# Operand addresses by padding, one merged first load, and a prioritised evacuation in a one-core decoder layer

## Chip, core and metric

The kernel runs on one NeuronCore of a Trainium2 chip. The metric is the device time of one execution in microseconds; several runs of the same kernel are compared by their median.

## What is computed

One decoder layer over 256 tokens of width 2048, all in fp32. A combined projection feeds two attentions (multi-head latent attention with 16 heads, sliding-window attention with 32 query heads and 4 key/value heads), whose outputs are gated, merged and projected; a gated feed-forward with a causal convolution of width 3 follows.

```
h  = RMSNorm_pre(x)
P  = h @ W_in        # 2048 x 7488: q-latent | kv-latent | rope key | q, k, v of the window | two gates
A  = latent attention(P) ; Bq = window attention(P)
y  = W_out( sigmoid(gA) * (A @ Wo_A) + sigmoid(gB) * (Bq @ Wo_B) )
x  = x + RMSNorm_post(y)
x  = x + RMSNorm_post2( ConvFFN( RMSNorm_pre2(x) ) )   # 2048 -> 2 x 5632 -> 2048
```

## The kernel before

Every matrix product is done with three fp32r matmuls. Each operand is split into a high part (a cast to fp32r) and a low part (the remainder), and `mm3` (L144 to L147) issues high x high, low x high and high x low into one PSUM accumulator. The weight is the moving operand (512 columns in most products), the activations are the stationary operand (128 columns: one of two token tiles).

`gemm` (L149) walks the contraction dimension in chunks of two k-tiles of 128 rows (512 KB). For each chunk `wchunk` (L103) issues one DMA on SP's queue into a `raw` buffer (`RAW` = 3 of them), lets ScalarE cast it to `whi` (L120) and VectorE form `wlo` (L121); `whi` and `wlo` have five buffers each (`RING`). Each k-tile then has two token tiles with three matmuls each, so a chunk of two k-tiles is 12 matmuls.

The stationary activations stand in tiles of 128 x 512 fp32r: `ah`/`al` (slots "a": normalised x, later the merged branch and the first 8 of 12 feed-forward tiles), `bh`/`bl` (slots "b": the window attention's output, the latent attention's output, the second normalised x) and `gh`/`gl` (the other four feed-forward tiles, from a later pool). In the down projection (`down`, L902) a product's contraction therefore runs first over `ah`/`al` and then over `gh`/`gl`, with the same weights' buffers as moving operand.

Where a tile stands in SBUF follows from the order in which the pools hand out space. Three dummy tiles shift everything behind them: `line_a` (L233, `LINE_A` columns) stands ahead of slots a, `line_b` (L335) ahead of slots b, `line_w` (L339) ahead of the weights' ring and all later pools. The start addresses in one partition, in bytes, as the built programs have them:

| tiles | first address before, modulo 256 | first address after, modulo 256 |
|---|---|---|
| `ah`, `al` | 21760, 0 | 21984, 224 |
| `bh`, `bl` | 54784, 0 | 55008, 224 |
| `raw`, `whi`, `wlo` | 87936, 128 | 88288, 224 |
| `gh`, `gl` | 191360, 128 | 191712, 224 |
| `cqh`, `ckh`, `qn`, `kn`, `kx` and others of the attentions | 0 | 96 |

Columns within a tile are reached in steps of 512, 1024, 1280 or 2048 bytes, so a slice has the residue of its tile.

The first product (`acc_kv`, L283: keys and values of the window attention) starts while x is still being loaded, in an order written by hand (up to `head.close()`). `load_xt` brings transposed pieces of x (1, 1, 2, 2, ... k-tiles), the first two and the norm scales `gmat` from ScalarE's queue, the others from SP's between the weights. `x_cols` splits each piece into `ah` and `al` with the norm scale, and asks for the next one. Untransposed x comes in four loads `xc`; their sums of squares (`x_square`) give the row factor `r1` (`x_norm`, L274), which is only applied when the accumulators are evacuated (`swa_kv`, L300): ScalarE and VectorE write the keys `kd`, ScalarE the values `vs`. TensorE then turns the values over with `flip` (`swa_v`, tile `vr`, L312) and transposes the keys (`swa_k`, tile `kt`, L319). These steps stand in a list by chunk (`at`, `tick`): `swa_begin` after chunk 2 of the next product, `swa_kv` after 3, `swa_v` after 4 and 5, `swa_k` after 4 to 7. From there on a scheduler orders each engine's instructions by the program's order and by priorities.

Of the kernel before, what the change touches and what calls it, by code (L numbers as in the profile page):

```python
# [19 lines left out]
P = 128  # L20
D = 2048
S = 256
NT = 2
KT = D // P
# [14 lines left out]
GELU_C = math.sqrt(2.0 / math.pi)  # L39


def trunk_layer(ctx, tc, x, x_cols_in, gain_cols, conv_cols_in, g_mix_post, g_ffn_post, w_in, w_q, w_kv,
                sinks, rel, wo_a, wo_b, w_out, w_up, w_down, rope_tab, strip_sel, out):
    nc = tc.nc
    vec, act, pe, pool = nc.vector, nc.scalar, nc.tensor, nc.gpsimd
# [10 lines left out]
    base = ctx.enter_context(tc.tile_pool(name="base", bufs=1))  # L56
    ring = ctx.enter_context(tc.tile_pool(name="ring", bufs=RING))

    def sb(pl, shape, name, dt=F32, tag=None, bufs=None):
        return pl.tile(shape, dt, name=name, tag=tag or name, **({"bufs": bufs} if bufs else {}))  # L60
# [12 lines left out]
    def warm_up(n):  # L73
        for i in range(n):
            tc.keep_in_program_order(pe.matmul(warm[:, 0:P], ident_b, ident_b, start=True, stop=True))

    warm_up(WARM[0])
    causal = sb(base, [P, P], "causal", BF16)
# [10 lines left out]
    gmat = sb(base, [P, 38], "gmat")  # L89
# [13 lines left out]
    def wchunk(src, shape, own=None, rawp=None):  # L103
        i = cnt[0]
        cnt[0] += 1
        n = int(np.prod(shape))
        raw = rawp.tile([P, 1024], F32, name=f"raw{i}", tag="xraw") if rawp else \
            ring.tile([P, 1024], F32, name=f"raw{i}", tag="raw", bufs=RAW)
        dst = raw[:, :n]
        if len(shape) == 2:  # L110
            dst = dst.rearrange("p (a b) -> p a b", a=shape[0])
        elif len(shape) == 3:
            dst = dst.rearrange("p (a b c) -> p a b c", a=shape[0], b=shape[1])
        if len(shape) == 3:
            for k in range(shape[0]):
                nc.sync.dma_start(dst[:, k], src[:, k])
        else:
            nc.sync.dma_start(dst, src)
        hi, lo = ((own or ring).tile([P, 1024], F32R, name=f"w{part}{i}", tag="w" + part) for part in ("hi", "lo"))
        act.copy(hi[:, :n], raw[:, :n])  # L120
        vec.tensor_tensor(lo[:, :n], raw[:, :n], hi[:, :n].bitcast(F32), op=ALU.subtract)  # L121
        return hi, lo
# [5 lines left out]
    def at(t, *fs):  # L128
        steps[max(t, now[0])].extend(fs)

    def tick():
        for f in steps.pop(now[0], ()):
            f()
        now[0] += 1
# [5 lines left out]
    def new_acc(tag):  # L140
        i = cnt[0]
        return [pacc.tile([P, 512], F32, name=f"acc{tag}_{i}_{t}", tag="acc") for t in range(NT)]

    def mm3(o, ah, al, bh, bl, start, stop):  # L144
        pe.matmul(o, ah, bh, start=start, stop=False)  # L145
        pe.matmul(o, ah, bl, start=False, stop=False)  # L146
        pe.matmul(o, al, bh, start=False, stop=stop)  # L147

    def gemm(xh, xl, w, k0, nk, c0, n, split=False, pre=None, extra=None):  # L149

        kc = 1024 // n if n in (256, 512) else 2
        acc = new_acc("g")
        todo = []
        cuts = [0, 1, 2] + list(range(4, nk + 1, 2)) if pre else list(range(0, nk, kc)) + [nk]
        for ci, (k, ke) in enumerate(zip(cuts[:-1], cuts[1:])):
            kk = ke - k
            src = w[(k0 + k) * P:(k0 + k + kk) * P, c0:c0 + n].rearrange("(a p) n -> p a n", p=P)
            if pre and ci == 0:
                pre(k, ke)
            hi, lo = wchunk(src, [kk, n], *(extra or {}).get(ci, ()))  # L160
            if pre and ke < nk:
                pre(ke, cuts[ci + 2])
            for j in range(kk):
                kt = k + j
                wh, wl = hi[:, j * n:(j + 1) * n], lo[:, j * n:(j + 1) * n]
                for t in range(NT):
                    def go(kt=kt, t=t, wh=wh, wl=wl):
                        mm3(acc[t][:, :n], xh(k0 + kt)[:, t * P:(t + 1) * P],
                            xl(k0 + kt)[:, t * P:(t + 1) * P], wh, wl, kt == 0, kt == nk - 1)
                    if split and t == 1:  # L170
                        todo.append(go)
                    else:
                        go()
            tick()
        return acc, todo
# [23 lines left out]
    def split_to(hi, lo, src, scale=None):  # L199

        if scale is None:
            act.copy(hi, src)  # L202
            vec.tensor_tensor(lo, src, hi.bitcast(F32), op=ALU.subtract)
        else:
            act.activation(hi, src, AF.Copy, scale=scale)
            vec.scalar_tensor_tensor(lo, src, scale, hi.bitcast(F32), op0=ALU.mult, op1=ALU.subtract)
# [1 line left out]

    esl, lpool = open_pool("lpool")
    es0, p0 = open_pool("p0")  # L210
    xcut = [0, 1, 2] + list(range(4, KT + 1, 2))
    xr = sb(p0, [P, KT, 256], "xr")

    def load_xt(i, q):
        if i < len(xcut) - 1:
            k, ke = xcut[i], xcut[i + 1]
            q.dma_start(xr[:, k:ke, :], x_cols_in[:, k * 256:ke * 256].rearrange("p (k n) -> p k n", n=256))

    first = sb(base, [P, 1], "first")
    nc.scalar.dma_start(gmat, gain_cols)  # L220
    load_xt(0, nc.scalar)
    load_xt(1, nc.scalar)
    act.copy(first, ident[:, 0:1])
    xc = []

    def load_x():
        c = len(xc)
        t = sb(p0, [P, NT, 512], f"xc{c}")
        nc.sync.dma_start(t, x[:, c * 512:(c + 1) * 512].rearrange("(t p) n -> p t n", p=P))
        xc.append(t)  # L230

    cvT = sb(base, [P, 176], "cvT")
    sb(base, [P, LINE_A], "line_a")  # L233
    xth = [slot_a(p, "h") for p in range(8)]
    xtl = [slot_a(p, "l") for p in range(8)]
    XH, XL = pair_view(xth), pair_view(xtl)
# [9 lines left out]
            act.activation(junk, xc[c][:, t, :], AF.Square, accum_out=ssx[:, t, c:c + 1])  # L246

    def x_cols(k, ke):
        i = xcut.index(k)
        if i:  # L250
            load_xt(i + 1, nc.sync)
        if i in (5, 6, 7):
            load_x()
        if i == 8:
            x_square(0)
        for k in range(k, ke):
            split_to(XH(k), XL(k), xr[:, k, :], gmat[:, k:k + 1])


    strip = dram.tile([SH, 384], F32, name="strip")  # L260
# [13 lines left out]
    def x_norm():  # L274
        vec.tensor_reduce(v1, ssx, axis=AX.X, op=ALU.add)
        vec.tensor_scalar(v1, v1, 1.0 / D, EPS, op0=ALU.mult, op1=ALU.add)
        r = rsqrt(v1, NT, "r1", base)
        vec.tensor_scalar(r1s, r, 0.125, None, op0=ALU.mult)
        vec.tensor_scalar(rh, r, 0.5, None, op0=ALU.mult)
        return r  # L280

    warm_up(WARM[1])
    acc_kv, _ = gemm(XH, XL, w_in, 0, KT, C_KS, 512, pre=x_cols)  # L283
    load_x()
    head.close()

    es1, p1, r1, kx, vx, kd, vs = None, None, None, [], [], [], []

    def swa_begin():
        nonlocal es1, p1, r1
        x_square(3)
        r1 = x_norm()
        es0.close()
        es1, p1 = open_pool("p1")
        kx.extend(sb(p1, [P, 2, 384], f"kx{g}", F32R) for g in range(4))
        vx.extend(sb(p1, [P, 4, 2, 64], f"vx{t}", F32R) for t in range(NT))

    def swa_kv(t):  # L300
        kk = sb(p1, [P, 4, 2, 64], f"kd{t}", tag="qx", bufs=2)
        a3 = acc_kv[t].rearrange("p (a b) -> p a b", b=64)
        act.activation(kk[:, :, 0, :], a3[:, 0:4, :], AF.Copy, scale=r1[:, t:t + 1])
        vec.tensor_scalar(kk[:, :, 1, :], a3[:, 0:4, :], r1[:, t:t + 1], None, op0=ALU.mult)
        v_ = sb(p1, [P, 256], f"vs{t}", tag="p", bufs=3)
        act.activation(v_, acc_kv[t][:, 256:512], AF.Copy, scale=r1[:, t:t + 1])
        kd.append(kk)
        vs.append(v_)

    def swa_v(t):  # L310
        pv_ = pss.tile([P, 512], F32, name=f"vr{t}", tag="s")
        pe.matmul(pv_[:, 0:256], flip, vs[t], start=True, stop=True)  # L312
        o = pv_[:, 0:256].rearrange("p (a b) -> p a b", b=64)
        split_to(vx[t][:, :, 0, :], vx[t][:, :, 1, :], o)
# [13 lines left out]
    at(2, swa_begin)  # L328
    for t in range(NT):
        at(3, lambda t=t: swa_kv(t))  # L330
        at(4 + t, lambda t=t: swa_v(t))
    for g in range(4):
        at(4 + g, lambda g=g: swa_k(g))

# [3 lines left out]
    OH, OL = pair_view(oth), pair_view(otl)  # L338
    sb(base, [P, LINE_W], "line_w")  # L339

# [478 lines left out]
    for b in range(4):  # L819
        c0, n = W_BLOCKS[b]  # L820
# [114 lines left out]
    for b in range(NB):  # L935
        c0, n = blocks[b]
# [15 lines left out]


RING = 5
WARM = (12, 15)
EXTRA = 3
LINE_A = 24
LINE_B = 32
LINE_W = 8
RAW = 3  # L960
STG = 4

# [27 lines left out]
def _columns(a):  # L990

    return np.asarray(a).reshape(-1, P).T
# [32 lines left out]
```

## Time and profile before

| | us |
|---|---|
| median of 3 runs | 1524.61 (1523.99 to 1525.87) |
| the profiled execution's own time | 1525.49 |
| its span, first to last instruction | 1523.7 |
| TensorE busy in it (matmuls) | 1507.3 |
| VectorE busy, ScalarE busy | 940.2, 799.8 |
| mean granted TensorE clock | 0.998 |

Matmuls overlap their neighbours in the trace: a matmul's own duration says less than the distance from one start to the next. That distance is read from a stretch's length and its number of weight loads, one for each matmul.

### The profile page before, as it was taken

What the parts mean: (1) busy time and instruction counts of PE and PEld (TensorE: products, weight loads), DVE (VectorE), ACT (ScalarE), POOL (GpSimd) and SP (SyncE); (2) the same over time, 40 slices, a digit from 0 to 9 for tenths busy, and PEclk for the clock granted to TensorE, in tenths of its full rate; (3) what the DMA queues carried; (4) which work ended last, traced back from release to release, by engine and by line L of the source; (5) the groups of instructions that cost most, each with busy time, mean ns of one, the idle gap of its engine ahead of it and who ended that gap; (6) DMA issues with size and microseconds to landing.
All of it is one profiled execution on the core that took longest, in us unless ns stands there. A gap on an engine that the chain in (4) does not pass through costs nothing.

```text
span 1523.7 us, 20082 instructions
## 1 busy us (share of the span) xinstructions
PE 1507.3 (99%) x7311; PEld 1246.1 (82%) x7311; DVE 940.2 (62%) x1603; ACT 799.8 (52%) x1290; POOL 59.1 (4%) x99
## 2 busy tenths in 40 slices
PE   9999999999999999999999999999999999999997
PEld 7788888888889888888888888888888888888887
DVE  6688884445676665655766656666444466656755
ACT  6588874434565553444655545555443455545542
POOL 1022200000000010000000000000000000000000
PEclk9999999999999999999999999999999999999999
DMA  9776566666655558766555566655556665655563
GB/s 302 209 188 170 146 187 184 205 205 197 180 162 148 176 175 306 240 203 194 175 186 179 179 185 187 179 180 181 186 189 193 184 184 180 184 180 180 180 192 112
DMA packets 162979, 287.55 MB, mean 189 GB/s; under 512 B 18613, under 2 KB 34261, under 8 KB 162752
## 3 DMA queue, kind: packets, MB, share of 16 engines
q1 hardware_dynamic: 157440, 269.78, 57.5%
q0 software_dynamic: 5008, 16.21, 4.2%
q8 instruction: 57, 0.93, 0.2%
q14 instruction: 42, 0.34, 0.1%
q10 hardware_dynamic: 432, 0.28, 0.1%
HBM read 279.89 MB, written 6.34 MB: 188 GB/s over the span
## 4 chain that ended last, share of the span: by engine, by line
PE 94%; DVE 2%; ACT 2%; DMA 1%; issue 1%; DVEq 0%; ACTq 0%; SPq 0%
PE accg L145 28%; PE accg L146 28%; PE accg L147 28%; PE fT L850 1%; DMA raw<-in_w_in_dram 1%; PE mpo L684 1%; PE ms L650 1%; DVE wlo L121 1%; PE qn L613 0%; PE qn L615 0%; PE qn L614 0%; ACT p L410 0%; PE pt L368 0%; PE ms L655 0%; ACT whi L120 0%
## 5 line engine op out<-in xcount | busy, mean ns | idle before, releaser
L121 DVE TENSOR_TENSOR wlo<-raw,whi 128x1024 fp32r<-128x1024 f32 (+2 forms) x501 | 609.0, 1217 | 509.6 <-ACT whi L120 509.3
L120 ACT CAST whi<-raw 128x1024 fp32r<-128x1024 f32 (+2 forms) x501 | 522.1, 1043 | 616.5 <-PE accg L147 528.8
L145 PE MATMUL accg<-whi,bh 128*128 128x512 f32 x960 | 382.6, 399 | 0.0
L147 PE MATMUL accg<-whi,bl 128*128 128x512 f32 x960 | 379.1, 395 | 0.0
L146 PE MATMUL accg<-wlo,bh 128*128 128x512 f32 x960 | 379.0, 395 | 0.0
L145 PE MATMUL accg<-whi,ah 128*128 128x512 f32 (+2 forms) x896 | 347.8, 389 | 1.1 <-ACT whi L120 1.1
L146 PE MATMUL accg<-wlo,ah 128*128 128x512 f32 (+2 forms) x896 | 345.8, 386 | 0.0
L147 PE MATMUL accg<-whi,al 128*128 128x512 f32 (+2 forms) x896 | 344.9, 385 | 0.0
L147 PEld LDWEIGHTS accg<-whi,bl 128*128 128x128 f32 x960 | 180.4, 188 | 43.0
L146 PEld LDWEIGHTS accg<-wlo,bh 128*128 128x128 f32 x960 | 180.6, 188 | 41.1
L145 PEld LDWEIGHTS accg<-whi,bh 128*128 128x128 f32 x960 | 180.5, 188 | 40.8
L147 PEld LDWEIGHTS accg<-whi,al 128*128 128x128 f32 x896 | 169.3, 189 | 35.1
L145 PEld LDWEIGHTS accg<-whi,ah 128*128 128x128 f32 x896 | 169.4, 189 | 33.7 <-ACT whi L120 1.4
L146 PEld LDWEIGHTS accg<-wlo,ah 128*128 128x128 f32 x896 | 169.4, 189 | 33.6 <-DVE wlo L121 0.7
L145 PE MATMUL accg<-whi,gh 128*128 128x512 f32 (+1 forms) x104 | 39.4, 378 | 0.0
L146 PE MATMUL accg<-wlo,gh 128*128 128x512 f32 (+1 forms) x104 | 38.8, 373 | 0.0
L147 PE MATMUL accg<-whi,gl 128*128 128x512 f32 (+1 forms) x104 | 38.4, 374 | 0.0
L410 ACT ACTIVATE p<-p,nm 128x128 f32<-128x128 f32 x64 | 28.3, 445 | 5.8 <-DVE nm L401 5.8
L850 PEld LDWEIGHTS fT<-ident,f 128*128 128x128 f32 x176 | 21.9, 141 | 6.0
L850 PE MATMUL fT<-ident,f 128*128 128x128 f32 x176 | 26.4, 272 | 0.0
L854 ACT ACTIVATE cc<-fT,cvT 128x256 f32<-128x256 f32 x44 | 24.3, 553 | 0.0
L145 PEld LDWEIGHTS accg<-whi,gh 128*128 128x128 f32 x104 | 19.6, 188 | 4.1 <-ACT gh L202 0.8
(289 smaller groups left out, 1265.6 us busy)
## 6 DMA issues: line engine op xcount, KB each, us to landing
raw<-in_ffn_w_up_dram SPq DMA_DIRECT2D x176, 512.0 KB, 4.1
raw<-in_w_in_dram SPq DMA_DIRECT2D x111, 512.0 KB, 4.3
raw<-in_ffn_w_down_dram SPq DMA_DIRECT2D x88, 512.0 KB, 3.8
raw<-in_w_o_swa_dram SPq DMA_DIRECT2D x32, 512.0 KB, 4.1
raw<-in_w_o_mla_dram SPq DMA_DIRECT2D x32, 512.0 KB, 4.5
raw<-in_w_out_dram SPq DMA_DIRECT2D x32, 512.0 KB, 4.0
raw<-in_mla_w_q_up_dram SPq DMA_DIRECT2D x48, 128.0 KB, 2.6
bias<-strip POOLq DMA_DIRECT2D x16, 256.0 KB, 3.9
```

The lines of the kernel that those rows point to most:

```text
L120: act.copy(hi[:, :n], raw[:, :n])
L121: vec.tensor_tensor(lo[:, :n], raw[:, :n], hi[:, :n].bitcast(F32), op=ALU.subtract)
L145: pe.matmul(o, ah, bh, start=start, stop=False)
L146: pe.matmul(o, ah, bl, start=False, stop=False)
L147: pe.matmul(o, al, bh, start=False, stop=stop)
L410: act.activation(pb[:, i, a:b], pb[:, i, a:b], AF.Exp, bias=st["nm"][:, i, t:t + 1], accum_out=st["sm"][:, i, t:t + 1])
L650: pe.matmul(o, w, v_, start=n == 0, stop=False)
L684: pe.matmul(o, w(t), p_[:, c], start=n == 0, stop=n == 5)
L850: pe.transpose(pt[:, q * 256 + t * P:q * 256 + (t + 1) * P], sa[t][q][:, i * P:(i + 1) * P], ident)
L854: act.activation(cc, a, AF.Identity, scale=w2, bias=cb_)
```

## The change

The pads `LINE_A` and `LINE_W` become larger, which gives the addresses in the table above. The norm scales and the first k-tile of x become one input array and one load (`gx`); `gmat` is copied out of it later by GpSimd. All pieces of x come on SP's queue, in the order in which they are used; the first six k-tiles of x and of the weight come singly (before: two). The loads `xc` come one piece later. `x_norm` and `swa_kv` get a higher priority, and `swa_v` moves two chunks later (`swa_k` stays where it is).

```diff
-    nc.scalar.dma_start(gmat, gain_cols)
-    load_xt(0, nc.scalar)
-    load_xt(1, nc.scalar)
+    gx = sb(p0, [P, 38 + 256], "gx")
+    xr = [sb(p0, [P, ke - k, 256], f"xr{k}") for k, ke in zip(XCUT[1:-1], XCUT[2:])]
+    def load_xt(i):
+        if i == 0:
+            nc.sync.dma_start(gx, x_cols_in[:, 0:38 + 256])
+        elif i < len(XCUT) - 1:
+            k, ke = XCUT[i], XCUT[i + 1]
+            nc.sync.dma_start(xr[i - 1], x_cols_in[:, 38 + k * 256:38 + ke * 256].rearrange("p (k n) -> p k n", n=256))
+    load_xt(0)
...
     def x_cols(k, ke):
-        i = xcut.index(k)
-        if i:
-            load_xt(i + 1, nc.sync)
-        if i in (5, 6, 7):
+        i = XCUT.index(k)
+        for j in {0: (), 1: (1, 2)}.get(i, (i + 1,)):
+            load_xt(j)
+        if i in X_AT:
             load_x()
-        if i == 8:
+        if i == len(XCUT) - 2:
             x_square(0)
-        for k in range(k, ke):
-            split_to(XH(k), XL(k), xr[:, k, :], gmat[:, k:k + 1])
+        for j in range(k, ke):
+            src = xr[i - 1][:, j - k, :] if i else gx[:, 38:]
+            split_to(XH(j), XL(j), src, gx[:, j:j + 1])
...
     load_x()
+    pool.tensor_copy(gmat, gx[:, 0:38])
     head.close()
...
-        r1 = x_norm()
+        with tc.high_priority(300):
+            r1 = x_norm()
...
     def swa_kv(t):
+        with tc.high_priority(300):
+            swa_evac(t)
+
+    def swa_evac(t):
...
-        at(4 + t, lambda t=t: swa_v(t))
+        at(6 + t, lambda t=t: swa_v(t))
...
+XCUT = [0, 1, 2, 3, 4, 5, 6, 8, 10, 12, 14, 16]
+X_AT = (8, 9, 10)
-LINE_A = 24
+LINE_A = 80
 LINE_B = 32
-LINE_W = 8
+LINE_W = 40
```

More of the change, by code (lines that the diff above doesn't have):

```diff
@@ L39, with trunk_layer @@
 GELU_C = math.sqrt(2.0 / math.pi)
-def trunk_layer(ctx, tc, x, x_cols_in, gain_cols, conv_cols_in, g_mix_post, g_ffn_post, w_in, w_q, w_kv,
+def trunk_layer(ctx, tc, x, x_cols_in, conv_cols_in, g_mix_post, g_ffn_post, w_in, w_q, w_kv,
                 sinks, rel, wo_a, wo_b, w_out, w_up, w_down, rope_tab, strip_sel, out):
@@ L153, in gemm @@
         todo = []
-        cuts = [0, 1, 2] + list(range(4, nk + 1, 2)) if pre else list(range(0, nk, kc)) + [nk]
+        cuts = XCUT if pre else list(range(0, nk, kc)) + [nk]
         for ci, (k, ke) in enumerate(zip(cuts[:-1], cuts[1:])):
@@ L210, in trunk_layer @@
     es0, p0 = open_pool("p0")
[L211 to L217, printed above, removed]
+    gx = sb(p0, [P, 38 + 256], "gx")
[6 more added lines that the diff above has]
+            nc.sync.dma_start(xr[i - 1], x_cols_in[:, 38 + k * 256:38 + ke * 256].rearrange("p (k n) -> p k n", n=256))
     first = sb(base, [P, 1], "first")
-    nc.scalar.dma_start(gmat, gain_cols)
-    load_xt(0, nc.scalar)
-    load_xt(1, nc.scalar)
+    load_xt(0)
     act.copy(first, ident[:, 0:1])
@@ L1009 @@
         add(name, inputs[name], name != "rel_bias_table")
-    add("x_cols", np.asarray(inputs["x"])[0].T.reshape(KT, P, S).transpose(1, 0, 2).reshape(P, KT * S), False)
-    add("gain_cols", np.concatenate([_columns(inputs[n][0]) for n in
-                                     ("norm_mix_pre", "norm_ffn_pre", "mla_q_norm", "mla_kv_norm")], 1), False)
+    gains = [_columns(inputs[n][0]) for n in ("norm_mix_pre", "norm_ffn_pre", "mla_q_norm", "mla_kv_norm")]
+    cols = np.asarray(inputs["x"])[0].T.reshape(KT, P, S).transpose(1, 0, 2).reshape(P, KT * S)
+    add("x_cols", np.concatenate(gains + [cols], 1), False)
     add("conv_cols", np.concatenate([_columns(inputs["ffn_conv_w"][0]), _columns(inputs["ffn_conv_b"][0])], 1), False)
@@ L1017 @@
     o = nc.dram_tensor("out_0_dram", (1, S, D), F32, kind="ExternalOutput").ap()
-    order = ["x", "x_cols", "gain_cols", "conv_cols", "norm_mix_post", "norm_ffn_post", "w_in", "mla_w_q_up", "mla_w_kv_up",
+    order = ["x", "x_cols", "conv_cols", "norm_mix_post", "norm_ffn_post", "w_in", "mla_w_q_up", "mla_w_kv_up",
              "swa_sinks", "rel_bias_table", "w_o_mla", "w_o_swa", "w_out", "ffn_w_up", "ffn_w_down", "rope_tab", "strip_sel"]
```

## The prediction

> **What bounds the kernel now.** I read the page first, then the groups of TensorE by shape, the table by stretches, the waits of TensorE, and the timeline of the start.
>
> ```profile
> span 1523.7 us, 20082 instructions
> PE 1507.3 (99%) x7311; PEld 1246.1 (82%) x7311; DVE 940.2 (62%) x1603; ACT 799.8 (52%) x1290; POOL 59.1 (4%) x99
> PE 94%; DVE 2%; ACT 2%; DMA 1%; issue 1%; DVEq 0%; ACTq 0%; SPq 0%
> ```
>
> TensorE is busy for 99% of the span, and the chain that ended last runs over it for 94%. Nothing but shorter matmul work or a shorter start can move the end by much. The groups by shape (engine, operation, tiles, shape, count, busy us, mean ns):
>
> ```profile
> L145 PE MATMUL accg<-whi,bh 128*128 128x512 f32 x960 | 382.6, 399 | 0.0
> L145 PE MATMUL accg<-whi,ah 128*128 128x512 f32 x800 | 319.6, 400 | 1.1 <-ACT whi L120 1.1
> L146 PE MATMUL accg<-wlo,gh 128*128 128x512 f32 x88 | 34.3, 390 | 0.0
> ```
>
> Each stands for three rows of the same count, one for each line of `mm3`. So 3 x 960 + 3 x 800 = 5280 matmuls of 512 columns have their stationary operand in `a` or `b` tiles (0 modulo 256), and 3 x 88 = 264 have it in `g` tiles (128). The moving operand is at 128 for all of them. Their means overlap, so the time that each takes from the next is read from stretches. The next table has a stretch on `bh` tiles, then twice the two halves of one down product, first over `ah`, then over `gh`; 96 or 48 weight loads (PEld, x) are 96 or 48 matmuls:
>
> ```profile
> core 0: us, PE busy (x) PEld busy (x) DVE busy (x) ACT busy (x) POOL busy (x), PEclk, DMA share, GB/s
> 253.99:276.29 22.30, 22.30 (x97) 18.09 (x96) 10.08 (x9) 9.16 (x10) 0.00 (x0) 1.00 0.65 191
> 1102.69:1125.01 22.32, 22.32 (x97) 18.09 (x96) 10.49 (x9) 8.50 (x9) 0.00 (x0) 1.00 0.60 191
> 1125.01:1135.92 10.91, 10.91 (x49) 9.01 (x48) 4.90 (x4) 4.69 (x5) 0.00 (x0) 1.00 0.60 188
> 1135.92:1158.23 22.32, 22.32 (x97) 18.09 (x96) 10.49 (x9) 8.50 (x9) 0.00 (x0) 1.00 0.61 191
> 1158.23:1169.15 10.92, 10.92 (x49) 9.01 (x48) 4.90 (x4) 4.70 (x5) 0.00 (x0) 1.00 0.68 190
> ```
>
> 22.32 / 96 = 232.5 ns from matmul to matmul with stationary at 0 (`bh`: 232.3), but 10.915 / 48 = 227.4 ns with stationary at 128, where both operands have the same residue. Clock, DMA and the neighbours' load (VectorE 47% and 45%, ScalarE 38% and 43%) hardly differ. So 5.1 ns of each matmul, 2.2%, go with the place of the stationary tile. This is the row on which most of the forecast rests.
>
> **The change part by part.** *Pads.* Afterwards stationary and moving operand of all 5544 matmuls have the same residue, 224, as `gh` and `whi` have now at 128. I take the price of the row that is like it: 5280 x 5.1 ns = 26.9 us gained; nothing for the 264. The trace has no operand at 224, so the ends are: upward 0.24 us per matmul, which single matmuls take now (below), downward a second step of 5.1 ns. The products with 256 columns get nothing: their operands keep the distance of 128 bytes (96 against 224) or the order below shows no difference.
>
> ```profile
> L145 PE MATMUL accg<-whi,ah 128*128 128x256 f32 x64 | 18.0, 281 | 0.0
> L145 PE MATMUL accg<-whi,gh 128*128 128x256 f32 x16 | 4.5, 282 | 0.0
> ```
>
> Not all stretches can use faster matmuls. From 186 to 229 us the chain goes through loads, casts and VectorE:
>
> ```profile
> 186.00:229.00 43.00, 41.88 (x234) 35.84 (x233) 35.03 (x103) 31.63 (x71) 4.04 (x4) 1.00 0.58 174
> 197.32 4.45 DMA raw<-in_w_in_dram
> 214.29 4.35 DMA raw<-in_w_in_dram
> ```
>
> There a shorter interval only turns into waiting for the next `raw` or split: 2.2% of 43 us, 0.9 us given back. Elsewhere casts and loads keep ahead (VectorE 62%, ScalarE 52%), so the weights aren't late next. Sum for the pads: -26.0 us.
>
> *Evacuation of k and v.* In the waits of TensorE one stall in mid-run stands out; the timeline shows its cause:
>
> ```profile
> PE vr L312 <- issue: 1.9, 1, 1.9
> 44.09 1.05 ACT L120 CAST whi<-raw 128x1024 fp32r<-128x1024 f32 x1 [4.34 <-PE accg L147]
> 45.04 0.83 ACT L303 ACTIVATE kd<-accg,r_y 128x256 f32<-128x256 f32 x2
> 47.26 1.04 ACT L120 CAST whi<-raw 128x1024 fp32r<-128x1024 f32 x1 [1.38 <-DMA raw<-in_w_in_dram]
> 48.21 0.83 ACT L306 ACTIVATE vs<-accg,r_y 128x256 f32<-128x256 f32 x2
> 48.77 0.67 PE L312 MATMUL vr<-vs,flip 128*128 128x256 f32 x2 [1.89 <-issue]
> 41.51 0.16 DVE L196 SCALAR_TENSOR_TENSOR r_y<-r_u,r_y 128x2 f32<-128x2 f32 x1
> ```
>
> `vr` waits 1.89 us for `vs`, which stands on ScalarE behind two casts, one of which waits 4.34 us for a free buffer. The row factor was there at 41.67. In the changed program `kd` stands one cast earlier, directly behind that factor on VectorE, and `vr` two chunks later (some 24 matmuls, 5.5 us). What is late next is `kt`, which needs `kd`: done near 43, wanted near 47. The cast put behind `kd` waited for TensorE anyway. `xc` loads come a chunk (2.8 us) later and delay the factor, but its small steps no longer stand between splits of the weights. I take -1.9 us; the other end, `kd` late by one load, is +1.0.
>
> *Start.*
>
> ```profile
> 2.05 3.06 PE L75 MATMUL warm<-ident_b 128*128 128x128 bf16 x27 [2.05 <-DVE ident_b L70]
> 5.14 0.51 ACT L205 ACTIVATE ah<-xr,gmat 128x256 fp32r<-128x256 f32 x1 [1.49 <-DMA xr<-in_x_cols_dram]
> 5.55 0.60 ACT L120 CAST whi<-raw 128x512 fp32r<-128x512 f32 x1
> 6.19 0.69 DVE L121 TENSOR_TENSOR wlo<-raw,whi 128x512 fp32r<-128x512 f32 x1
> 6.21 0.79 PE L145 MATMUL accg<-whi,ah 128*128 128x512 f32 x1 [1.10 <-ACT whi L120]
> 1.67 0.42 SPq L118 DMA_DIRECT2D raw<-in_w_in_dram  x1
> raw<-in_w_in_dram SPq DMA_DIRECT2D x2, 256.0 KB, 4.1
> 9.23 0.63 PE L145 MATMUL accg<-whi,ah 128*128 128x512 f32 x1
> 9.66 0.63 PE L146 MATMUL accg<-wlo,ah 128*128 128x512 f32 x1
> 12.91 0.39 PE L145 MATMUL accg<-whi,ah 128*128 128x512 f32 x1
> 13.14 0.39 PE L146 MATMUL accg<-wlo,ah 128*128 128x512 f32 x1
> 5.00:13.00 8.00, 6.90 (x17) 5.00 (x17) 5.43 (x10) 6.08 (x12) 0.00 (x0) 1.00 1.00 346
> ```
>
> The first x lands at 5.1, among everything else; the DMA engines are full (share 1.00). Alone at the head of the queue it comes earlier, but the 27 warm-up matmuls end at 5.1, so at most 1.1 us of idle goes. Up to about 12.7 matmuls follow each other in 0.43 us (9.23 to 9.66), later in 0.23 (12.91 to 13.14). If that slow time ends when it does now, an earlier start gains only (1 - 0.23/0.43), about half. Against it: single k-tiles fill the three `raw` buffers with half the bytes. Queue entries cost SP some 0.85 us per k-tile (two of 0.42), under the 6 x 0.23 = 1.4 us that TensorE needs, but a buffer's round of landing (4.1), cast (0.6) and split (0.7) through three buffers is 1.8 us per k-tile, more than 1.4; over three fast k-tiles that costs up to 1.2 us, and the slow ones before (2.6 us each) build some lead. I take -0.7, between -1.5 (idle and the small gaps behind it) and +1.2. The copy of `gmat` on GpSimd stands ahead of the `strip` store on its queue, which waits for VectorE anyway: nothing.
>
> Sum: -26.0 - 1.9 - 0.7 = -28.6 us. The profiled execution took 1525.49 us (span 1523.7 and 1.8 around it), 0.9 above the median; on the median, 1524.61 - 28.6 = **1496**, with 1490 to 1506 from the ends of start and evacuation and 1 ns (5.3 us) either way on the interval.
>
> **Rivals.** *Place, not residue.* `gh` differs from `ah` also in lying above 191,000 bytes, far from the weights' ring, where `ah` lies below it. If distance makes the 5.1 ns, the pads give nothing, and 1524.6 - 1.9 - 0.7 = 1522 remains. For it: `bh` and `ah`, 32 KB apart, both take 232 ns; against it: both have residue 0 as well. The Trainium skill speaks for this rival too: SBUF — State Buffer, "Who interferes with whom", gives TensorE two independent read ports, one for the moving operand and one for weight loads, and says that it never waits on anyone; by that, residues would not matter. The trace disagrees at least so far that 232.5 and 227.4 stand side by side in one product.
>
> *Slower: 224 is a bad residue.* Starts 0.24 us apart occur now:
>
> ```profile
> 1150.33 0.40 PE L147 MATMUL accg<-whi,al 128*128 128x512 f32 x1
> 1150.57 0.40 PE L145 MATMUL accg<-whi,ah 128*128 128x512 f32 x1
> 1150.81 0.40 PE L146 MATMUL accg<-wlo,ah 128*128 128x512 f32 x1
> ```
>
> Both operands now begin 32 bytes (8 columns) before a 256-byte boundary and meet the next block together. If each matmul then takes 240 instead of 232.5 ns, 5280 x 7.5 = 40 us are lost, and the time is 1562; it decides from 233 ns on. Against it: sharing a residue did no harm at 128.
>
> *More than `gh` shows.* If 224 takes off a second step of the same size, 5544 x 5.1 = 28 us more, 1468. The trace has no sign of it. The Trainium skill, TensorE: Matmul & The Clock Gate, "Back-to-back issue gap", gives N / 2.4 + 2.5 ns, 216 ns for 512 columns; an estimate by it would be about 1432. No stretch here comes under 227.
>
> **How the numbers follow.** Forecast 0.55, place 0.16, slower 0.12, more 0.17. A measurement of this kernel tells about 0.2% (3 us) from no change. Of the place case, 1522 with the start's ends, 0.05 is counted as faster and 0.11 as the same. Faster 0.55 + 0.17 + 0.05 = 0.77, same 0.11, slower 0.12. The range leaves out the slower case and the lower half of "more": 1474 to 1523.
>
> **What would show it.** In the same down product the stretches over `ah` and over `gh` should both take about 227 ns per weight load; 232 for `ah` alone is the place rival, 233 or more for both the bad residue. The wait before `vr` should be gone and none stand before `kt`. The first `accg` should start between 5.1 and 5.7, with no TensorE idle before 20 us from late `whi`. The forecast is wrong if the interval isn't near 227 ns.

## The result and the profile after

| | before | after |
|---|---|---|
| median, same chip | 1525.24 us (1523.99 to 1528.08, 4 runs) | 1502.55 us (1501.49 to 1505.37, 4 runs) |
| the profiled execution, its span | 1525.49, 1523.7 | 1502.2, 1500.4 |

The ratio is 0.9852, 95% interval 0.9832 to 0.9871: 22.7 us faster (19.7 to 25.6 by the interval), where 28.6 were forecast. From the page of the changed kernel:

```profile
span 1500.4 us, 20098 instructions
PE 1481.6 (99%) x7311; PEld 1241.7 (83%) x7311; DVE 940.7 (63%) x1605; ACT 801.8 (53%) x1292; POOL 59.4 (4%) x100
PE 89%; DMA 4%; DVE 3%; ACT 3%; issue 1%; SPq 0%; DVEq 0%; ACTq 0%
```

TensorE is still busy for 99%, with the same 7311 matmuls in 25.7 us less. On the chain of waits its share falls from 94% to 89%, and DMA's rises from 1% to 4%: part of what the matmuls gave up has become waiting for loads. The groups by shape:

```profile
L145 PE MATMUL accg<-whi,bh 128*128 128x512 f32 x960 | 378.3, 394 | 0.0
L145 PE MATMUL accg<-whi,ah 128*128 128x512 f32 x800 | 315.6, 395 | 2.0 <-ACT whi L120 2.0
L146 PE MATMUL accg<-wlo,ah 128*128 128x512 f32 x800 | 313.7, 392 | 2.8 <-DVE wlo L121 2.6
L146 PE MATMUL accg<-wlo,gh 128*128 128x512 f32 x88 | 34.3, 389 | 0.0
```

`bh` and `ah` went from 399 and 400 ns to 394 and 395; `gh` stayed (390 to 389). The stretches as the prediction read them, on `bh`, then over `ah`, `gh`, `ah`, `gh` of one down product (same columns; PEld's count is the matmuls):

```profile
254.78:276.54 21.76, 21.76 (x98) 18.02 (x96) 10.01 (x9) 9.21 (x10) 0.00 (x0) 1.00 0.67 194
1087.74:1109.50 21.76, 21.76 (x97) 18.02 (x96) 10.49 (x9) 8.55 (x9) 0.00 (x0) 1.00 0.63 195
1109.50:1120.38 10.88, 10.88 (x49) 9.01 (x48) 4.90 (x4) 4.70 (x5) 0.00 (x0) 1.00 0.61 191
1120.38:1142.14 21.76, 21.76 (x97) 18.02 (x96) 10.49 (x9) 8.55 (x9) 0.00 (x0) 1.00 0.63 195
1142.14:1153.02 10.88, 10.88 (x49) 9.01 (x48) 4.90 (x4) 4.70 (x5) 0.00 (x0) 1.00 0.68 194
```

21.76 / 96 = 10.88 / 48 = 226.7 ns everywhere: one interval for all, 5.7 ns below the 232.4 of before, and also 0.7 below the 227.4 of `gh` before. The start and the middle tell another story. The waits of TensorE in the first 75 us, then four stretches (5 to 13, 5 to 40, 40 to 75, 75 to 240 us), first of the changed kernel, then the same stretches of before:

```profile
PE accg L146 <- DVE wlo L121: 2.6, 6, 0.6
PE accg L145 <- ACT whi L120: 2.0, 3, 1.1
PE kt L327 <- DVE kx L203: 0.6, 1, 0.6
5.00:13.00 8.00, 6.70 (x27) 4.63 (x26) 4.81 (x10) 4.21 (x9) 0.00 (x0) 1.00 0.83 244
5.00:40.00 35.00, 30.80 (x121) 21.31 (x120) 21.28 (x37) 22.31 (x45) 4.07 (x6) 1.00 0.89 294
40.00:75.00 35.00, 33.54 (x169) 27.43 (x169) 22.57 (x41) 19.80 (x29) 0.74 (x2) 1.00 0.77 230
75.00:240.00 165.00, 163.24 (x877) 137.02 (x877) 135.86 (x423) 132.58 (x328) 33.22 (x44) 1.00 0.65 172
```

```profile
5.00:40.00 35.00, 33.90 (x131) 26.06 (x131) 23.31 (x39) 24.91 (x46) 4.07 (x6) 1.00 0.93 312
40.00:75.00 35.00, 33.12 (x169) 27.47 (x168) 21.92 (x41) 19.65 (x35) 1.41 (x2) 1.00 0.73 214
75.00:240.00 165.00, 163.40 (x873) 136.45 (x872) 135.94 (x419) 130.89 (x321) 32.48 (x43) 1.00 0.64 172
```

The wait before `vr` is gone. But by 40 us the changed kernel has done 120 matmuls and the kernel before 131, some 2.4 us less work, with new waits for `wlo` and `whi`. From 40 to 240 us it does 6 more. So the gain comes after 240 us.

### The profile page after: what moved, and what is told of

It reads as the page before. It is cut to its first block, busy times and chain, and to the rows that moved or that the text cites. A ratio compares the mean times of both kernels' runs of the same rounds, so it can differ in the third digit from the quotient of the medians.

```text
span 1500.4 us, 20098 instructions
## 1 busy us (share of the span) xinstructions
PE 1481.6 (99%) x7311; PEld 1241.7 (83%) x7311; DVE 940.7 (63%) x1605; ACT 801.8 (53%) x1292; POOL 59.4 (4%) x100
## 4 chain that ended last, share of the span: by engine, by line
PE 89%; DMA 4%; DVE 3%; ACT 3%; issue 1%; SPq 0%; DVEq 0%; ACTq 0%
PE accg L145 27%; PE accg L147 26%; PE accg L146 26%; DMA raw<-in_w_in_dram 4%; PE fT L858 1%; DVE wlo L121 1%; ACT whi L120 1%; PE mpo L692 1%; PE ms L658 1%; ACT p L418 1%; PE qn L621 1%; PE qn L623 1%; PE qn L622 1%; PE ms L663 0%; PE ptm L376 0%
## 5 line engine op out<-in xcount | busy, mean ns | idle before, releaser
L145 PE MATMUL accg<-whi,bh 128*128 128x512 f32 x960 | 378.3, 394 | 0.0
L147 PE MATMUL accg<-whi,bl 128*128 128x512 f32 x960 | 374.5, 390 | 0.0
L146 PE MATMUL accg<-wlo,bh 128*128 128x512 f32 x960 | 373.6, 389 | 0.0
L145 PE MATMUL accg<-whi,ah 128*128 128x512 f32 (+2 forms) x896 | 343.8, 385 | 2.0 <-ACT whi L120 2.0
L146 PE MATMUL accg<-wlo,ah 128*128 128x512 f32 (+2 forms) x896 | 341.9, 382 | 2.8 <-DVE wlo L121 2.6
L147 PE MATMUL accg<-whi,al 128*128 128x512 f32 (+2 forms) x896 | 340.7, 380 | 0.0
```

## The experiments

Two theories of the pads stood: equal residues of both operands make the interval short (any residue, if equal), or the place of the tile, or the residue 224, does. For the 5.9 us missing from the forecast: the start loses, the pads give less, or the evacuation does.

**The pads alone.** The kernel before with

```diff
-LINE_A = 24
+LINE_A = 80
-LINE_W = 8
+LINE_W = 40
```

> The kernel before with the two pads alone (LINE_A 80, LINE_W 40), loads and evacuation as before. If the pads carry the gain: 226.7 ns per matmul in the down product over ah and over gh, and a time of 1524.6 - 26 = 1498 to 1500. If part of the gain comes from the new start (the changed kernel was 2 us behind at 240 us, so this would be a surprise): 1503 or more. If the wider misplacement of the loaded tiles slows the loads, the changed kernel's loss of 2 us up to 100 us shows here too, with the old order of loads.

Measured: 1502.18 us (1500.81 to 1503.10), before 1524.28; ratio 0.9853, interval 0.9839 to 0.9868. The interval came out as expected, the time 2 us above the expected 1498 to 1500. The pads alone gain 22.1 us, as much as the whole change within the intervals. The stretches over `ah` and `gh` (96 and 48 matmuls) are within 0.01 us of those of the changed kernel:

```profile
1085.89:1107.64 21.75, 21.75 (x97) 18.02 (x96) 10.49 (x9) 8.54 (x9) 0.00 (x0) 1.00 0.60 194
1107.65:1118.52 10.87, 10.87 (x49) 9.01 (x48) 4.90 (x4) 4.70 (x5) 0.00 (x0) 1.00 0.61 194
```

What the interval can't move shows in the next two stretches:

```profile
5.00:40.00 35.00, 32.16 (x133) 23.98 (x132) 23.14 (x38) 24.63 (x46) 4.07 (x6) 1.00 0.93 309
75.00:240.00 165.00, 162.50 (x875) 136.43 (x874) 136.09 (x419) 131.19 (x321) 32.50 (x43) 1.00 0.63 173
```

From 75 to 240 us 874 matmuls are done instead of 872. TensorE's busy time falls by 0.9 us, which turned into gaps; VectorE stays at 136 and ScalarE at 131 of 165 us. The chain of waits over these 165 us points the same way: each of the three `accg` lines falls from 14% to 9%, the landings of `raw` rise from 8.2% to 10.7%, `wlo` from 5.0% to 6.5%:

```profile
by line: PE accg L146 14.2%; PE accg L147 14.1%; PE accg L145 14.1%; DMA raw<-in_w_in_dram 8.2%; DVE wlo L121 5.0%; issue 4.3%; ACT p L410 4.3%; PE pt L368 4.1%; ACT whi L120 3.4%; PE s L390 3.0%; PE xp L358 2.1%; DVE o L444 2.0%; DVE ptl L
```

```profile
by line: DMA raw<-in_w_in_dram 10.7%; PE accg L146 9.2%; PE accg L147 9.2%; PE accg L145 9.0%; ACT p L410 7.0%; DVE wlo L121 6.5%; issue 6.5%; ACT whi L120 4.8%; DVE ptl L203 2.9%; DVE o L444 2.8%; PE xp L358 2.3%; PE pt L368 2.2%; ACT p L4
```

(The first row is the kernel before, the second the pads alone.)

**Everything but the pads.** The changed kernel with `LINE_A = 24`, `LINE_W = 8`.

> The changed kernel with the pads of before (stationary at 0, moving at 128). Theory: start and evacuation together gain nothing, since raw tiles come late between 15 and 65 us: 1525 to 1528, 232.5 ns per matmul over ah. By the prediction's terms (evacuation -1.9, start -0.7): 1522. If the pads are what slows the loads of the start, this one keeps the early first matmul and ends at 1520 to 1522.

Measured: 1525.43 us (10 runs), ratio 1.0005, interval 0.9996 to 1.0015. Start and evacuation together give nothing (-0.6 to +2.3 us by the interval, against -2.6 by the prediction's terms). By the starts of the same matmul in both traces, it is 2.0 us behind before at 39 us, level at 53, 1.1 behind at 73 and 0.1 behind at the end. Two stretches, over `ah` and over `gh`, are as before (22.32 / 96 = 232.5); the first row is the start, from 5 to 13 us:

```profile
5.00:13.00 8.00, 7.62 (x28) 5.47 (x27) 5.03 (x10) 4.13 (x9) 0.00 (x0) 1.00 0.89 271
1102.81:1125.13 22.32, 22.32 (x98) 18.11 (x96) 10.50 (x9) 8.50 (x9) 0.00 (x0) 1.00 0.59 190
1125.13:1136.04 10.91, 10.91 (x49) 9.01 (x48) 4.90 (x4) 4.70 (x5) 0.00 (x0) 1.00 0.59 189
```

**Other equal residues.** The kernel before with only the pads changed: all of `ah`, `bh`, `gh`, `whi` at 0 (`LINE_W = 40`), and all at 128 (`LINE_A = 56`, `LINE_W = 40`).

> The kernel before with LINE_W 40 alone: weights' tiles at 0 modulo 256, a, b and g tiles at 0 too. If the same residue of both operands is what counts: 227 ns over ah and gh. If residue 0 of the stationary operand is what costs: 232 ns over both. If the place far from the weights counts: 232 over ah, 227 over gh.

> The kernel before with LINE_A 56 and LINE_W 40: a, b, g tiles and weights all at 128 modulo 256. Same residue: 227 ns over ah and gh, as gh has it in the kernel before (227.4). Residue 0 bad: also 227. If only 224 is good, ah stays at 230 or more.

Measured: 1500.53 and 1498.82 us, one run each. Over `ah`, at 0 and then at 128:

```profile
1085.43:1107.19 21.76, 21.76 (x97) 18.03 (x96) 10.49 (x9) 8.55 (x9) 0.00 (x0) 1.00 0.59 193
```

```profile
1083.98:1105.73 21.75, 21.75 (x97) 18.02 (x96) 10.49 (x9) 8.54 (x9) 0.00 (x0) 1.00 0.58 194
```

226.6 to 226.7 ns in both. 224 has no virtue of its own. With all at 0, `ah` stands at the very address of the kernel before, where it took 232.5; only the weights' ring and the pools behind it have moved by 128 bytes. The theory of place falls.

**224 against 96.** `LINE_A = 80` alone: `ah`, `bh` at 224, the weights and `gh` at 96.

> The kernel before with LINE_A 80 alone: a and b tiles at 224, weights at 96 (128 bytes apart modulo 256), g tiles at 96 as the weights. If the distance counts: 232 ns over ah, 227 over gh, 1522 to 1526 in all. If a stationary operand at 224 is good by itself: 227 over both and about 1502.

Measured: 1525.53 us, one run.

```profile
1102.68:1125.00 22.32, 22.32 (x98) 18.09 (x96) 10.50 (x9) 8.50 (x9) 0.00 (x0) 1.00 0.63 190
1125.00:1135.91 10.91, 10.91 (x49) 9.01 (x48) 4.90 (x4) 4.70 (x5) 0.00 (x0) 1.00 0.58 189
```

The old 232.5 over `ah`, 227.3 over `gh`, whose residue is that of the weights: new residues, old distance, old price.

**Smaller distances.** `LINE_W = 56` puts the weights and `gh` at 64, `LINE_W = 48` at 32; `ah` and `bh` stay at 0.

> The kernel before with LINE_W 56: the a and b tiles at 0, the weights and g tiles at 64 modulo 256. If only equal residues modulo 256 avoid the cost: 230 to 234 ns per matmul over ah, 227 over gh (whose tiles have the residue of the weights), 1515 to 1526 us. If equality modulo 64 is enough: 226.7 over both, about 1500 us.

> The kernel before with LINE_W 48: the a and b tiles at 0, the weights and g tiles at 32 modulo 256. If any distance costs the same: 232.5 ns over ah. If the cost grows with the distance: 227 to 230. If 32 bytes are near enough: 226.7. Over gh 226.7 to 227.5 in each case.

Measured: 1509.43 and 1525.48 us, one run each (the kernel before next to them: 1527.46, one run). Over `ah` and `gh`, at a distance of 64, then of 32:

```profile
1092.89:1114.85 21.96, 21.96 (x97) 18.02 (x96) 10.50 (x9) 8.47 (x9) 0.00 (x0) 1.00 0.62 193
1114.86:1125.73 10.87, 10.87 (x49) 9.01 (x48) 4.90 (x4) 4.70 (x5) 0.00 (x0) 1.00 0.60 189
```

```profile
1102.77:1125.16 22.39, 22.39 (x98) 17.99 (x96) 10.49 (x9) 8.47 (x9) 0.00 (x0) 1.00 0.60 189
1125.16:1136.04 10.88, 10.88 (x49) 9.01 (x48) 4.90 (x4) 4.70 (x5) 0.00 (x0) 1.00 0.59 191
```

21.96 / 96 = 228.8 ns at 64, 22.39 / 96 = 233.2 at 32, and 226.5 to 226.7 over `gh`. Neither expectation for 64 held (230 to 234, or 226.7): its price is 2.1 ns, that of 32 is 6.5, that of 128 is 5.8. Distance has a price that neither grows nor falls evenly; only 0 is free among those tried. Each price is read from one trace.

**Pads and evacuation, with the old start.** The pads, and

```diff
-        r1 = x_norm()
+        with tc.high_priority(300):
+            r1 = x_norm()
...
-        at(4 + t, lambda t=t: swa_v(t))
+        at(6 + t, lambda t=t: swa_v(t))
```

with the same priority around `swa_kv`; then the same with all tiles at 128.

> The kernel before with the pads (80, 40) and the evacuation's part (priority of x_norm and swa_kv, swa_v two chunks later); loads as before. The wait of vr (2.3 us with the pads alone) should go. If nothing takes its place: 1502.2 - 2 = 1500. If the next step waits instead (kt for kd or kx) or the stretch up to 230 us, which loads and casts set, takes it back: 1502, no difference from the pads alone.

> As e5, but all operands at 128 instead of 224 modulo 256. If only the distance of the two residues counts: 226.7 ns per matmul and the same time as e5 within 1 us. If tiles at 224 cost something else (loads of the weights into them, casts): 1.5 to 3 us less than e5.

Measured: 1499.47 us (1498.72 to 1500.34), ratio 0.9836, interval 0.9822 to 0.9849; and 1498.80 us (1497.82 to 1500.32), ratio 0.983, interval 0.9817 to 0.9843. By their medians both are 3 to 4 us ahead of the changed kernel, by the ratios 2.4 and 3.4 us, but the intervals overlap with its own; between the two no difference can be told. The first of them:

```profile
PE kt L324 <- issue: 0.4, 1, 0.4
5.00:13.00 8.00, 6.46 (x16) 4.13 (x15) 4.60 (x8) 5.38 (x10) 0.00 (x0) 1.00 0.95 324
5.00:40.00 35.00, 33.46 (x130) 24.99 (x129) 23.13 (x38) 24.23 (x46) 4.07 (x6) 1.00 0.92 307
40.00:75.00 35.00, 34.47 (x175) 28.62 (x174) 22.36 (x44) 21.08 (x38) 1.41 (x2) 1.00 0.75 224
```

From 40 to 75 us it does 174 matmuls where the pads alone do 169: 5 x 0.23 = 1.2 us from the evacuation in the trace; by the two ratios 0.9853 and 0.9836 it is 2.6 us, but each has an interval of 2 us on either side, and the intervals overlap. The other pair shows no gain: with all at 128 the time was 1498.82 us without the evacuation's part (one run) and 1498.80 with it. By the starts of the same matmul, the run with it gains 1.0 us on the other from 39 to 73 us and has lost 0.8 of that by 245. So the removed wait is shown, and what it is worth in the end is not.

**The new start with the old pieces.** The changed kernel with

```diff
-XCUT = [0, 1, 2, 3, 4, 5, 6, 8, 10, 12, 14, 16]
-X_AT = (8, 9, 10)
+XCUT = [0, 1, 2, 4, 6, 8, 10, 12, 14, 16]
+X_AT = (6, 7, 8)
```

run twice, because its first profile had half the granted clock from 12.4 to 19.2 us.

> The changed kernel with the pieces of before (1, 1, 2, 2, ... k-tiles) instead of six single ones; everything else as changed. If the single pieces starve the three raw buffers: the first 40 us come out some 2 us shorter than in the changed kernel, 1500 to 1501. If the order of the loads on the one queue or the later xc loads do it: 1502.5 as the changed kernel, with the same lag at 40 us.

> The kernel of e7 once more, for a profile of its start without the halved clock. If single pieces of x starve the raw buffers: level with the kernel before or ahead of it at 39 us (the changed kernel is ahead by 2.4 us less than that: it is 2.4 us behind). If the one queue or the later loads of xc do it: some 2 us behind again.

Measured: 1500.88 us (1499.23 to 1502.20, 4 runs), ratio 0.9842, interval 0.9829 to 0.9856; the second time 1501.06. The second profile has the half clock again (PEclk, third column from the right, second row):

```profile
5.00:13.00 8.00, 4.30 (x15) 2.23 (x13) 3.52 (x7) 3.33 (x7) 0.00 (x0) 0.94 1.01 308
13.00:20.00 7.00, 7.00 (x19) 5.52 (x20) 5.46 (x9) 5.53 (x9) 0.00 (x0) 0.58 0.92 304
5.00:40.00 35.00, 31.30 (x119) 23.54 (x118) 19.89 (x31) 22.00 (x43) 4.07 (x6) 0.90 0.92 307
```

With pairs the loads run at 308 GB/s from 5 to 13 us (changed kernel 244, before 346) and at the share of before up to 40 us (0.92 against 0.93; changed kernel 0.89). The run without the pads, which has single pieces too, went with 271 GB/s, and a share of 0.89 up to 40 us. So single pieces do lower the rate of the loads. That they cost the time isn't shown. The expected lead at 39 us did not come: the two profiles are 3.2 and 2.8 us behind. The half clock takes part of that, but by the matmul that starts at 13 us in the kernel before, they are already 1.7 and 1.3 us behind (the changed kernel is 2.2 ahead there), after TensorE had waited 1.9 and 1.7 us for one `whi`. By 73 us they are 0.8 and 0.2 behind, the changed kernel 2.2, and the time is 1.7 us below that of the changed kernel, with intervals that overlap. The rival of the expectation, the one queue or the later loads of `xc`, stays open.

## Why the prediction was right, and where not

*The mechanism and the row it rested on: right.* The forecast took the 5.1 ns between `ah` and `gh` for a matter of residues against place, against a bad 224 and against a second step. Equal residues at 0, 128 and 224 give one interval; unequal ones, at old or new addresses, cost. The place rival fell with the tiles at 0, the slower rival (240 ns at 224) with 226.7, and so did the second step of 5.1. The Trainium skill's rule in SBUF — State Buffer, "Who interferes with whom", that matmul and weight load read through independent ports, doesn't foresee this: with one pad moved, the same instructions take 232.5 or 226.7 ns.

*The interval: undersized in the stretches quoted.* 5.7 ns instead of 5.1, since `gh` before wasn't yet at the floor: 0.03 to 0.04 us longer per stretch than in the changed kernel. Why is open; it is there in the run of 224 against 96 too, and neither with all at one residue nor at a distance of 32 or 64 (10.88 and 10.87). 5280 x 5.7 = 30.1 us, where the prediction had 26.9.

*What is given back: undersized, the main miss of the pads.* Counted in the trace, 236 of the 5280 matmuls lie ahead of 73 us, 494 from there to 245, 4550 behind: 1.3, 2.8 and 25.9 us at 5.7 ns. The lead of the pads alone grew by 0.4, 0.5 and 23.8 us (from the same matmul in both traces): 24.7 in all, 5.4 below 30.1, where 0.9 was to be given back. This has two parts. Ahead of 245 us 3.2 us are missing. The step that failed there is "elsewhere casts and loads keep ahead (VectorE 62%, ScalarE 52%)": that was the mean of the run, and from 75 to 240 us VectorE is busy for 136 of 165 us (82%) and ScalarE for 131 (79%), so far more than 186 to 229 was bound elsewhere.

The other 2.1 us are missing behind 245 us, where the list of waits of TensorE is empty in both traces. There the mean gain is 23.8 us / 4550 = 5.2 ns, not 5.7; between 300 and 600 us, where 1.4 of the 2.1 are missing, 887 matmuls gain 3.6 us, 4.1 ns each. Why is open. That this mean is so near the 5.1 of the forecast is partly luck: the floor was lower than `gh` showed, and not every stretch reached it. By medians the pads gain 22.1; of the 2.6 between, 1.2 is how the profile of before (1525.49) stands above the median used (1524.28), 1.4 how that of the pads alone stands below its own.

*Evacuation: the wait right, the size open.* -1.9 was forecast; with the pads at 224, 1.2 in the trace and 2.6 by the ratios were measured, with all at 128 nothing. The wait before `vr` went as said. That none would stand before `kt` was wrong: 0.6 us with the change, 0.4 with the old start.

*Start: wrong sign.* Forecast -0.7, with +1.2 as its bad end. At 39 us the four traces with the new start are 2.0 to 3.2 us behind before, the eight others between 0.5 behind and 1.0 ahead. The first `accg` did come early, at 4.87 (before 6.21). But the prediction's sign of no idle before 20 us from late `whi` failed. The timeline of the changed kernel shows, by start and length:

```profile
5.44 0.33 SPq L118 DMA_DIRECT2D raw<-in_w_in_dram  x1
8.77 0.33 SPq L118 DMA_DIRECT2D raw<-in_w_in_dram  x1
4.87 0.78 PE L145 MATMUL accg<-whi,ah 128*128 128x512 f32 x1
7.40 0.62 ACT L120 CAST whi<-raw 128x512 fp32r<-128x512 f32 x1 [2.30 <-DMA raw<-in_w_in_dram]
8.07 0.50 PE L145 MATMUL accg<-whi,ah 128*128 128x512 f32 x1 [1.07 <-ACT whi L120]
```

For 3.3 us no DMA of weights is issued: all three `raw` buffers hold single k-tiles, and the next is free only when one has landed, been cast and split. Before, the same pause is longer (from 2.6 to 6.9 us), but the third buffer then holds a pair, 512 KB, and the pieces of x are pairs too, so the DMA engines stay full. With single pieces they fall to 0.83 and 244 GB/s; (346 - 244) x 8 us = 0.8 MB that weren't moved are 2.3 us at 350 GB/s. That is about the loss at 39 us (2.4). The prediction had this term, but weighed it against TensorE's need and not against the loads, which keep the DMA engines at a share of 0.89 to 0.93 up to 40 us and so bind the start. That the single pieces are the cause is argued from the rate and not shown, since the runs with pairs were behind at 39 us too. Its other assumption, that the slow time of matmuls ends at 12.7, didn't hold either, and the clock did not decide the lag: in the changed kernel matmuls stand 0.23 us apart from 6 us on (26 in 5 to 13 us), in the kernel with pads and evacuation in that stretch only 15, and by 40 us the latter is 9 ahead.

*The sum.* Pads 22.1 (26.0 forecast), evacuation 0 to 2.6 (1.9), start a loss (gain of 0.7 forecast). By the ratios of the changed kernel, 0.9852, and of the one without the new start, 0.9836, the start's loss is 2.4 us, but their intervals overlap. The firm figure is that of both together: without pads, start and evacuation come to +0.0005 of the time, and the -2.6 of the forecast lies outside the interval. By medians, 3.9 of the 5.9 us missing from the forecast are the pads' (22.1 for 26.0) and 2.0 those of the two others together (0.6 for 2.6).

## What to carry to other kernels

When a stream of fp32r matmuls like these stands above its floor, compare the start addresses of the stationary and the moving operand modulo 256, and pad one pool until they are equal; which residue they share didn't matter here. Value a faster interval only where TensorE ends the waits, stretch by stretch, not by the mean load of the other engines. In a start bound by loads, look at the rate of the loads before making the first pieces smaller: single ones with the same three buffers went with 244 and 271 GB/s here, pairs with 305 and 308. What this costs in time was not settled.

## What the runs showed of the hardware

The price of a distance isn't even: 0 bytes 0 ns, 32 bytes 6.5, 64 bytes 2.1, 128 bytes 5.8 per 512-column fp32r matmul. Why wasn't found out.

Equal residues end at 226.5 to 226.7 ns in the stretches quoted. The Trainium skill, TensorE: Matmul & The Clock Gate, "Back-to-back issue gap", gives 216 for an isolated matmul of 512 columns and 131 for a sustained stream; the lowest stretch quoted here is 10.87 / 48 = 226.5, so for such a stream the measured value is the one to reckon with.

By the granted clock in the records of the traces, full speed began at 12.7 us in the profile of before, at 5.7 in the changed kernel and in the pads alone, at 12.7 with pads and evacuation, at 5.1 with all at 128. Kernels with the same start got different times, so it isn't the kernel that sets it alone. Both profiles with pairs lost the full clock again at 12.1 to 12.4 us for 6.8 us, after TensorE had idled for loads (in one 4.30 busy of 8.00 us), and the profile at a distance of 64 lost it from 49.2 to 52.6 us, near the end of a wait of 3.1 us before `vr`. The Trainium skill, TensorE: Matmul & The Clock Gate, "What's actually happening", gives a free-running window of 3.4 us by which the clock is set, and a start of the full clock that varies by 0.5 us either way. The 6.8 and 3.4 us agree with two windows and one; the starts differ by far more here, from 4.9 us (distance 64) to 12.7.
